# Differential attention scores as 64-row products, the two components in the two halves of the array

## The chip, the cores and the metric

The kernel runs on one core of one Trainium2 chip. The metric is the time of one execution on the device in microseconds (us). A core has TensorE for matrix products, VectorE and ScalarE for element-wise work, GpSimd, and queues that start DMA transfers. In profiles TensorE's matmuls are "PE", its weight loads "PEld", VectorE is "DVE", ScalarE is "ACT", GpSimd is "POOL" and SyncE, which starts most DMAs, is "SP".

## The reference

A two-layer encoder trunk on 256 tokens of width 2048, in float32. Each layer normalises `x`, projects it with `w_in`, mixes it in three groups of heads (a gated convolution, differential attention, and cross-attention into 256 memory tokens), and adds the result times `w_out` to `x`. The change concerns the differential attention, 6 heads with two components of 64 columns each:

```python
q = rmsnorm(d_q.reshape(b, s, DIFF_HEADS, 2, DIFF_HALF_DIM), diff_q_norm_g[l])
k = rmsnorm(d_k.reshape(b, s, DIFF_HEADS, 2, DIFF_HALF_DIM), diff_k_norm_g[l])
...
sc = jnp.einsum('bhcqd,bhckd->bhcqk', qi, kt).astype(jnp.float32) * scale + bias[None, :, None]
p = jax.nn.softmax(sc, axis=-1).astype(vt.dtype)
o = jnp.einsum('bhcqk,bhkd->bhcqd', p, vt)
return o[:, :, 0] - lam.astype(o.dtype) * o[:, :, 1]
```

The sum over `d` of the scores has only 64 terms, separately for each component `c`.

## The kernel before

**Products in parts.** Every large product is made from two tiles per operand: `hi`, the operand cast to the matmul type, and `lo`, what the cast left out. `products` (line 305) issues three matmuls per tile of 128 rows: high by high, high by low, low by high. ScalarE makes `hi` (line 294), VectorE makes `lo` (line 295). These run in `block`, which walks over 16 row tiles of a weight matrix in 8 chunks of two and accumulates two tiles of 128 tokens x 512 columns in PSUM.

**The order of work.** Tracing goes through the blocks of `w_in` one after the other. Everything else is written as generators ("tasks"): after every chunk `run_side` steps those that are due. A number that a generator yields is the count of chunks until its next step. What has been produced is noted in the set `made`, and tasks that need it wait by yielding. `keep_in_program_order` (`pin`) puts an instruction behind the one traced before it on its engine; instructions that are not pinned may be reordered when the program is laid out.

**From projection to transposed parts.** For the first three blocks of group D (q and k of all heads), `normed` scales the accumulators, and the task `qk_T` turns the result so that channels lie on partitions: `turn_sheet` gives `whole`, whose 128 partitions are, for one head, the 64 channels of component 0 and below them the 64 of component 1. `qk_T` then writes the parts of q and k into `yT`, a tile of 2 x 16 x 256 on 128 partitions that later holds the layer's mixed output. It does so for each component `c` on 64 partitions at a time: for q the high part on the component's own half and the low part on the other half; for k the high part on both halves, and the low part on both halves, in `yT` for heads 0 to 3 and in a tile of its own, `k2` (tag `bgT`), for heads 4 and 5. Lines 551 and 552 make q's parts, lines 563 and 564 k's high part twice, lines 568 and 570 k's low part and its copy to the other half.

**Scores.** `diff_scores` makes one head: two PSUM tiles `s[0]` and `s[1]` (pool `ps_s`, two buffers), one for each component, of 128 queries x 2 x 256 keys. Since q's 128 partitions are high above low, and k's are the same part twice, one matmul of 128 rows adds two products: line 626 is (q high + q low) by k high, line 627 (q high + q low) by k low. Each is one weight load of 128 x 128 and 256 moving columns; a head takes 8. Afterwards VectorE adds the position bias to `s[0]` and `s[1]` (line 631), and ScalarE takes the exponentials (line 637). Heads go in pairs (`pair`), begun every `PAIR_EVERY` = 9 chunks from the fifth block of group D on, so their matmuls fall between those of line 305. Line 519 (`weighted`) multiplies the transposed weights with `v`, in matmuls of 128 moving columns. Line 134 transposes a 32-row tile of constants at the very start, and line 763 transposes 128-row tiles of the memory tokens.

Of the kernel before, what the change touches and what calls it, by code (L numbers as in the profile page):

```python
# [10 lines left out]
F32 = mybir.dt.float32  # L11
F32R = mybir.dt.float32r
I32 = mybir.dt.int32
AF = mybir.ActivationFunctionType
ALU = mybir.AluOpType
# [3 lines left out]
P = 128  # L19
D_MODEL = 2048  # L20
SEQ = 256
DEPTH = 2
NT = SEQ // P
# [4 lines left out]
CG = W_CONV // P  # L28
DH = W_DIFF // P
HALF = 64  # L30
# [18 lines left out]
def encoder(ctx: ExitStack, tc: tile.TileContext, x, mem, norm_g, w_in, conv_w, conv_b,  # L49
            dq_g, dk_g, lq1, lk1, lq2, lk2, head_g, mem_norm_g, w_mem_kv, mq_g, mk_g, w_out, out):  # L50
    nc = tc.nc
    x, mem, out = x[0], mem[0], out[0]

    def pool(name, bufs, space=None):
        kw = {"space": space} if space is not None else {}
        return ctx.enter_context(tc.tile_pool(name=name, bufs=bufs, **kw))
# [4 lines left out]
    keep = pool("keep", 1)  # L61
# [9 lines left out]
    def nm(s):  # L71
        uid[0] += 1
        return f"{s}_{uid[0]}"
# [71 lines left out]
    kgain = const.tile([P, DEPTH], F32, name="kgain")  # L145
# [64 lines left out]
    side, tasks = deque(), []  # L210
# [3 lines left out]
    def later(g, n):  # L214
        due[id(g)] = chunk[0] + n
        return g
# [235 lines left out]
    def normed(acc, gs, st, home):  # L452
        return normed_steps(nc.vector, acc, gs, st, home)
# [13 lines left out]
    def sheets(tag):  # L467
        return lambda: sheet(tmp if tag == "e" else keep, tag)
# [56 lines left out]

    def q_parts(yT, c, h):
        return yT[:, c, h, :]

    def k_first(yT, c, h):
        return yT[:, c, CG + h, :]

    def k_second(yT, k2, c, h):
        return yT[:, c, CG + DH + h, :] if h < 4 else k2[:, c, h - 4, :]

    ROWS = (slice(0, HALF), slice(HALF, P))

    def qk_T(l, yT, k2, nat, q, k):

        whole = yield from turn_sheet(nat)

        pin = tc.keep_in_program_order
        if q is not None:
            c0, h0, nh = q
            a = c0 // P
            for c in range(2):
                own, other = ROWS[c], ROWS[1 - c]
                src = whole[own, a:a + nh, :]
                hi = yT[own, c, h0:h0 + nh, :]  # L550
                pin(nc.scalar.copy(hi, src))
                pin(nc.vector.tensor_tensor(yT[other, c, h0:h0 + nh, :], src, hi.bitcast(F32), ALU.subtract))
                yield
            made.update(("q", l, h) for h in range(h0, h0 + nh))
        if k is not None:
            c0, h0, nh = k
            a = c0 // P
            for c in range(2):
                own, other = ROWS[c], ROWS[1 - c]
                src = whole[own, a:a + nh, :]  # L560
                g = kgain[own, l:l + 1]
                hi = yT[own, c, CG + h0:CG + h0 + nh, :]
                pin(nc.scalar.activation(hi, src, AF.Copy, scale=g))
                pin(nc.scalar.activation(yT[other, c, CG + h0:CG + h0 + nh, :], src, AF.Copy, scale=g))
                for at, n, dst, d0 in ((0, min(nh, 4 - h0), yT, CG + DH + h0), (4 - h0, h0 + nh - 4, k2, 0)):
                    if n > 0:
                        lo = dst[own, c, d0:d0 + n, :]
                        pin(nc.vector.scalar_tensor_tensor(lo, whole[own, a + at:a + at + n, :], g,
                                                           hi[:, at:at + n].bitcast(F32), ALU.mult, ALU.subtract))
                        pin(nc.scalar.copy(dst[other, c, d0:d0 + n, :], lo))  # L570
                yield
            made.update(("k", l, h) for h in range(h0, h0 + nh))

    scored = set()
# [41 lines left out]
            yield 1  # L616
        held["yn"] -= 1

    def diff_scores(l, h, yT, k2):
        while not {("q", l, h), ("k", l, h)} <= made:  # L620
            yield 1
        s = [ps_s.tile([P, NT, SEQ], F32, tag="s", name=nm("s")) for _ in range(2)]
        for c in range(2):
            for i in range(NT):
                qi = q_parts(yT, c, h)[:, i * P:(i + 1) * P]
                nc.tensor.matmul(s[c][:, i, :], qi, k_first(yT, c, h), start=True, stop=False)  # L626
                nc.tensor.matmul(s[c][:, i, :], qi, k_second(yT, k2, c, h), start=False, stop=True)  # L627
        scored.add((l, h))
        e = tmp.tile([P, 2, NT, SEQ], F32, tag="e", name=nm("e"))
        for c in range(2):  # L630
            nc.vector.scalar_tensor_tensor(e[:, c], dist, -slopes[h], s[c], ALU.mult, ALU.add)  # L631
        mx = small.tile([P, 2, NT], F32, tag="mx", name=nm("mx"))
        nc.vector.tensor_reduce(mx, e, AX.X, ALU.max, negate=True)  # L633
        sm = small.tile([P, 2, NT], F32, tag="sm", name=nm("sm"))
        for c in range(2):
            for i in range(NT):
                nc.scalar.activation(e[:, c, i], e[:, c, i], AF.Exp, bias=mx[:, c, i:i + 1],  # L637
                                     accum_out=sm[:, c, i:i + 1])
        iv = small.tile([P, 2, NT], F32, tag="iv", name=nm("iv"), bufs=6)
        nc.vector.reciprocal(iv, sm)  # L640
        cf = small.tile([P, NT], F32, tag="cf", name=nm("cf"))
        nc.vector.scalar_tensor_tensor(cf, sm[:, 0], neglam[:, l:l + 1], iv[:, 1], ALU.mult, ALU.mult)
        for i in range(NT):
            nc.vector.scalar_tensor_tensor(e[:, 0, i], e[:, 1, i], cf[:, i:i + 1], e[:, 0, i], ALU.mult, ALU.add)
        return e[:, 0], iv
        yield
# [183 lines left out]
    pin = tc.keep_in_program_order  # L830
# [205 lines left out]
    s = 1  # L1036
    while s < DEPTH * KT:
        l, k = divmod(s, KT)
# [22 lines left out]
        s = group[-1] + 1  # L1061

    for l in range(DEPTH):
        st = stats_of(ssx, "st")
# [3 lines left out]

        yT = T_tile("yT")
        yTs[l] = yT  # L1070
        k2 = keep.tile([P, 2, DH - 4, SEQ], F32R, tag="bgT", name=nm("k2"))

        def x_block(cols, order=ALLK, **how):
            return block(xT, w_in[l], cols, order, rows=x_row_tiles, **how)
# [1 line left out]
        def begin_pair(n, p):  # L1076
            tasks.append(later(p, max(1, start + PAIR_EVERY * n - chunk[0])))
# [4 lines left out]
        for b in order:  # L1082
            if b in begun:
                acc = x_block([(C_D + b * NB, NB)], ALLK[-QT:], acc=begun[b])
            else:
                acc = x_block([(C_D + b * NB, NB)], ready=m.ready if l == 0 and b == order[0] else None)
            if b == 3:
                v = keep.tile([P, NT, W_DIFF], F32, tag="v", name=nm("v"))
                ga = keep.tile([P, NT, W_DIFF], F32, tag="ga", name=nm("ga"))
            if b == 4:  # L1090
                start = chunk[0]
                for n in range(DH // 2):
                    begin_pair(n, pair((2 * n, 2 * n + 1), lambda h: diff_scores(l, h, yT, k2),
                                       (lambda h, yn, po, iv: diff_out(h, yn, po, iv, st, ga),
                                        lambda h, y: split_T(yT, CG + h, y, hgain[:, l:l + 1], pin=True)), v))
            if b < 3:
                tasks.append(later(qk_T(l, yT, k2, normed(acc, HALF, st, sheets(("mqT", "mga", "e")[b])),
                                 (0, 0, 4) if b == 0 else (0, 4, 2) if b == 1 else None,
                                 (256, 0, 2) if b == 1 else (0, 2, 4) if b == 2 else None), 8))
            else:  # L1100
                for t in range(NT):
                    if b == 3:
                        nc.scalar.activation(v[:, t, 0:NB], acc[t], AF.Copy, scale=col(st, R, t))
                    elif b == 4:
                        nc.scalar.activation(v[:, t, NB:768], acc[t][:, 0:256], AF.Copy, scale=col(st, R, t))
                        silu2(ga[:, t, 0:256], acc[t][:, 256:512], st, t)
                    else:
                        silu2(ga[:, t, 256:768], acc[t], st, t)

        mqT = keep.tile([P, MH, SEQ], F32, tag="mqT", name=nm("mqT"))  # L1110
        mga = sheet(keep, "mga")
        acc = x_block([(C_M, NB)])
# [7 lines left out]
        acc = x_block([(C_M + W_MEM, NB)])  # L1120
        for t in range(NT):
            a = tmp.tile([P, NB], F32, tag="nat", name=nm("a"), bufs=3)
# [10 lines left out]
        bgT = None  # L1133
# [53 lines left out]
        acc = x_block([(C_B, NB)])  # L1187
        scaled(both_rows(bg, 0, 4), acc, HR2)
        acc = x_block([(C_B + NB, 256), (C_G + NB, 256)])
        scaled(both_rows(bg, 4, 6), [a[:, 0:256] for a in acc], HR2)  # L1190
        gate(NB, 256, [a[:, 256:512] for a in acc])
        acc = x_block([(C_G, NB)])
        gate(0, NB, acc)
        tasks.append(later(turn_bg(list(range(CG))), 9))
        acc = x_block([(C_X, NB)])
        ux = sheet(keep, "bgx", CG)
        scaled(both_rows(ux, 0, 4), acc, R2)
        acc = x_block([(C_C, NB)])
# [13 lines left out]
        acc = x_block([(C_X + NB, 256), (C_C + NB, 256)])  # L1212
# [80 lines left out]
        acc = block(yT, w_out[l], [(3 * NB, NB)], rest, apart=4 if final else 0, acc=far, opened=(True, False))  # L1293
# [32 lines left out]
```

## Time and profile before

| | |
|---|---|
| time, median of 3 runs | 919.0 us (918.97 to 920.56) |
| the profiled execution: its own time | 919.16 us |
| the profiled execution: its span | 917.4 us |
| TensorE busy | 911.9 us, 4161 matmuls |
| TensorE weight loads busy | 757.3 us, 4161 loads |
| VectorE busy | 720.1 us, 1293 instructions |
| ScalarE busy | 515.8 us, 798 instructions |
| mean DMA rate | 235 GB/s |

The span runs from the first to the last instruction of the profiled execution. Busy time is the time in which at least one instruction of an engine was in progress; matmuls are pipelined, so each one's recorded length overlaps the next, and the time it really takes from the stream is the distance between starts. In the rows of groups the columns are line, engine, operation, tiles (written <- read), shape, count | busy time in us, mean length of one in ns | idle time before them in us and what ended it. In rows of the timeline they are start and length in us, engine, line, operation, tiles, shape, count. In rows of waits they are the total in us, the number of times, and the longest.

### The profile page before, as it was taken

The page shows a single profiled execution, that of the slowest core. Times are in us where ns is not written, and L with a number is a line of the kernel's source. Part 1 is how long each engine was busy: PE and PEld are TensorE (multiplying, and loading weights), DVE is VectorE, ACT ScalarE, POOL GpSimd, SP SyncE. Part 2 cuts the span into 40 slices and gives each one's busy share as a digit, 9 for nine tenths or more (in the row PEclk, how much of TensorE's full clock was granted, in tenths as well). Part 3 has the DMA queues.
Part 4 walks back from the last instruction along what each step waited for, and adds up shares of the span by engine and source line. Part 5 has one row for each costly group of instructions (what it writes and reads, how often), then busy time and mean ns, then how long its engine had stood idle before and what let it go on. Part 6 is the DMA issues. An engine that isn't in the chain of part 4 may idle for free.

```text
span 917.4 us, 12407 instructions
## 1 busy us (share of the span) xinstructions
PE 911.9 (99%) x4161; PEld 757.3 (83%) x4161; DVE 720.1 (78%) x1293; ACT 515.8 (56%) x798; POOL 38.3 (4%) x68
## 2 busy tenths in 40 slices
PE   9999999999999999999999999999999999999998
PEld 6888888888888888888888888888888888888887
DVE  5579978857799697677789857878898787588786
ACT  5667645675555556445556544578555565546352
POOL 2435010000000000000000000000000000000000
PEclk9999999999999999999999999999999999999999
DMA  8899878886679998979777867986889998968842
GB/s 288 289 243 248 287 247 229 244 222 197 188 206 238 247 256 235 263 243 241 264 215 228 275 203 213 268 239 178 236 231 221 266 260 227 268 215 234 275 161 92
DMA packets 244560, 215.15 MB, mean 235 GB/s; under 512 B 131976, under 2 KB 171720, under 8 KB 244496
## 3 DMA queue, kind: packets, MB, share of 16 engines
q1 hardware_dynamic: 239520, 208.71, 79.3%
q0 software_dynamic: 3776, 4.59, 2.1%
q10 hardware_dynamic: 1200, 1.07, 0.3%
q8 instruction: 32, 0.52, 0.2%
q14 instruction: 32, 0.26, 0.1%
HBM read 193.30 MB, written 21.00 MB: 234 GB/s over the span
## 4 chain that ended last, share of the span: by engine, by line
PE 99%; DMA 0%; ACT 0%; SPq 0%; DVE 0%; issue 0%; ACTq 0%
PE acc L305 92%; PE x L351 2%; PE po L519 1%; PE acc L351 1%; PE s L627 1%; PE po L749 1%; PE s L626 1%; PE acc L933 1%; PE pt L763 0%; DMA raw<-in_w_mem_kv_dram 0%; PE s L683 0%; PE s L681 0%; PE s L682 0%; PE rest L305 0%; ACT hi L915 0%; SPq L833 0%
## 5 line engine op out<-in xcount | busy, mean ns | idle before, releaser
L305 PE MATMUL acc<-hi,xT 128*128 128x512 f32 x1792 | 558.4, 390 | 0.0
L294 ACT CAST hi<-raw 128x1024 fp32r<-128x1024 f32 x270 | 283.9, 1053 | 277.3 <-PE acc L305 200.0
L295 DVE TENSOR_TENSOR lo<-raw,hi 128x1024 fp32r<-128x1024 f32 x270 | 329.0, 1222 | 126.7 <-ACT hi L294 124.5
L305 PEld LDWEIGHTS acc<-hi,xT 128*128 128x128 f32 x1792 | 336.3, 188 | 69.0
L305 PE MATMUL acc<-lo,xT 128*128 128x512 f32 x896 | 349.2, 390 | 0.0
L305 PEld LDWEIGHTS acc<-lo,xT 128*128 128x128 f32 x896 | 168.2, 188 | 33.6
L305 PE MATMUL acc<-hi,yT 128*128 128x512 f32 (+1 forms) x432 | 134.1, 388 | 0.0
L305 PEld LDWEIGHTS acc<-hi,yT 128*128 128x128 f32 x432 | 81.0, 188 | 16.7
L305 PE MATMUL acc<-lo,yT 128*128 128x512 f32 x216 | 83.7, 388 | 0.0
L305 PE MATMUL acc<-hi,memT 128*128 128x512 f32 x248 | 78.0, 392 | 0.0
L305 PEld LDWEIGHTS acc<-hi,memT 128*128 128x128 f32 x248 | 46.2, 188 | 9.3
L916 DVE SCALAR_TENSOR_TENSOR lo<-raw,cva,hi 128x1024 fp32r<-128x1024 f32 (+1 forms) x34 | 41.0, 1218 | 15.4 <-ACT hi L915 15.1
L305 PE MATMUL acc<-lo,memT 128*128 128x512 f32 x124 | 48.0, 391 | 0.0
L305 PEld LDWEIGHTS acc<-lo,yT 128*128 128x128 f32 x216 | 40.6, 188 | 8.4
L915 ACT ACTIVATE hi<-raw,cva 128x1024 fp32r<-128x1024 f32 (+1 forms) x34 | 36.5, 1101 | 12.4 <-DMA raw<-in_w_mem_kv_dram 12.2
L305 PEld LDWEIGHTS acc<-lo,memT 128*128 128x128 f32 x124 | 23.3, 188 | 5.5 <-DVE lo L916 0.8
L377 ACT CAST hi<-wide 128x1024 fp32r<-128x1024 f32 x15 | 15.6, 1050 | 16.3 <-DVE wide L380 6.9
L637 ACT ACTIVATE e<-e,mx 128x256 f32<-128x256 f32 x48 | 23.8, 500 | 1.4 <-DVE mx L633 1.3
L780 POOL DMA_DIRECT2D xt<-in_x_dram x32 | 21.5, 678 | 19.7 <-DVE rsy L189 13.6
L377 DVE TENSOR_TENSOR lo<-wide,hi 128x1024 fp32r<-128x1024 f32 x15 | 18.1, 1220 | 3.5 <-ACT hi L377 3.3
L264 ACT ACTIVATE xT<-xf,gx 128x256 fp32r<-128x256 f32 x32 | 14.3, 503 | 5.7 <-DVE xf L786 5.0
L631 DVE SCALAR_TENSOR_TENSOR e<-dist,s 128x512 f32<-128x512 f32 x24 | 15.7, 680 | 2.2 <-PE s L627 1.7
(210 smaller groups left out, 765.8 us busy)
## 6 DMA issues: line engine op xcount, KB each, us to landing
raw<-in_w_in_dram SPq DMA_DIRECT2D x192, 512.0 KB, 4.6
raw<-in_w_out_dram SPq DMA_DIRECT2D x54, 512.0 KB, 4.8
raw<-in_w_in_dram SPq DMA_DIRECT2D x64, 256.0 KB, 4.3
raw<-in_w_mem_kv_dram SPq DMA_DIRECT2D x30, 512.0 KB, 6.4
d<-sh SPq DMA_DIRECT2D x88, 128.0 KB, 4.2
sh<-d SPq DMA_DIRECT2D x72, 128.0 KB, 4.1
wide<-in_w_out_dram SPq DMA_DIRECT2D x10, 512.0 KB, 7.0
xs<-in_x_dram SPq DMA_DIRECT2D x4, 512.0 KB, 6.3
```

The source lines that it names most:

```text
L264: both = (nc.scalar.activation(hi, src, AF.Copy, scale=gain), nc.vector.scalar_tensor_tensor(lo, src, gain, hi.bitcast(F32), ALU.mult, ALU ...
L294: nc.scalar.copy(hi, raw)
L295: nc.vector.tensor_tensor(lo_, raw, hi.bitcast(F32), ALU.subtract)
L305: i = nc.tensor.matmul(acc, left, right, start=start, stop=stop)
L351: nc.tensor.matmul(acc, left[a], right[b], start=first and i == 0, stop=last and i == 2)
L377: return ((hi, pin(nc.scalar.copy(hi, src))), (lo, pin(nc.vector.tensor_tensor(lo, src, hi.bitcast(F32), ALU.subtract))))
L519: nc.tensor.matmul(po[:, t, :], eT[:, i, t, k, :], v[:, k, h * P:(h + 1) * P], start=k == 0, stop=k == NT - 1)
L631: nc.vector.scalar_tensor_tensor(e[:, c], dist, -slopes[h], s[c], ALU.mult, ALU.add)
L637: nc.scalar.activation(e[:, c, i], e[:, c, i], AF.Exp, bias=mx[:, c, i:i + 1], accum_out=sm[:, c, i:i + 1])
L780: tc.keep_in_program_order(nc.gpsimd.dma_start(st[:, n], src[n * B:(n + 1) * B].rearrange("p (b r) -> b p r", b=NA)))
L915: both = (nc.scalar.activation(hi[:, j], raw[:, j], AF.Copy, scale=g), nc.vector.scalar_tensor_tensor(lo[:, j], raw[:, j], g, hi[:, j].bit ...
L916: nc.vector.scalar_tensor_tensor(lo[:, j], raw[:, j], g, hi[:, j].bitcast(F32), ALU.mult, ALU.subtract))
```

## The change

`qk_T` writes q's high part to `yT[:, 0, h]` and its low part to `yT[:, 1, h]`, and k's likewise at index `CG + h`, in one instruction each over all 128 partitions, so that component 0 lies on partitions 0 to 63 and component 1 on 64 to 127. The part on the other half, the copies and the tile `k2` go, and with them one of the two `yield`s for q and one of the two for k. `diff_scores` forms each score tile from three products (high by high, high by low, low by high), the two components alternating: 12 matmuls of 64 rows a head, all pinned.

```diff
--- before.py
+++ after.py
@@ -525,50 +525,30 @@
 
 
 
-    def q_parts(yT, c, h):
-        return yT[:, c, h, :]
-
-    def k_first(yT, c, h):
-        return yT[:, c, CG + h, :]
-
-    def k_second(yT, k2, c, h):
-        return yT[:, c, CG + DH + h, :] if h < 4 else k2[:, c, h - 4, :]
-
     ROWS = (slice(0, HALF), slice(HALF, P))
 
-    def qk_T(l, yT, k2, nat, q, k):
+    def qk_T(l, yT, nat, q, k):
 
         whole = yield from turn_sheet(nat)
 
         pin = tc.keep_in_program_order
         if q is not None:
             c0, h0, nh = q
-            a = c0 // P
-            for c in range(2):
-                own, other = ROWS[c], ROWS[1 - c]
-                src = whole[own, a:a + nh, :]
-                hi = yT[own, c, h0:h0 + nh, :]
-                pin(nc.scalar.copy(hi, src))
-                pin(nc.vector.tensor_tensor(yT[other, c, h0:h0 + nh, :], src, hi.bitcast(F32), ALU.subtract))
-                yield
+            src = whole[:, c0 // P:c0 // P + nh, :]
+            hi = yT[:, 0, h0:h0 + nh, :]
+            pin(nc.scalar.copy(hi, src))
+            pin(nc.vector.tensor_tensor(yT[:, 1, h0:h0 + nh, :], src, hi.bitcast(F32), ALU.subtract))
+            yield
             made.update(("q", l, h) for h in range(h0, h0 + nh))
         if k is not None:
             c0, h0, nh = k
-            a = c0 // P
-            for c in range(2):
-                own, other = ROWS[c], ROWS[1 - c]
-                src = whole[own, a:a + nh, :]
-                g = kgain[own, l:l + 1]
-                hi = yT[own, c, CG + h0:CG + h0 + nh, :]
-                pin(nc.scalar.activation(hi, src, AF.Copy, scale=g))
-                pin(nc.scalar.activation(yT[other, c, CG + h0:CG + h0 + nh, :], src, AF.Copy, scale=g))
-                for at, n, dst, d0 in ((0, min(nh, 4 - h0), yT, CG + DH + h0), (4 - h0, h0 + nh - 4, k2, 0)):
-                    if n > 0:
-                        lo = dst[own, c, d0:d0 + n, :]
-                        pin(nc.vector.scalar_tensor_tensor(lo, whole[own, a + at:a + at + n, :], g,
-                                                           hi[:, at:at + n].bitcast(F32), ALU.mult, ALU.subtract))
-                        pin(nc.scalar.copy(dst[other, c, d0:d0 + n, :], lo))
-                yield
+            src = whole[:, c0 // P:c0 // P + nh, :]
+            g = kgain[:, l:l + 1]
+            hi = yT[:, 0, CG + h0:CG + h0 + nh, :]
+            pin(nc.scalar.activation(hi, src, AF.Copy, scale=g))
+            pin(nc.vector.scalar_tensor_tensor(yT[:, 1, CG + h0:CG + h0 + nh, :], src, g, hi.bitcast(F32),
+                                               ALU.mult, ALU.subtract))
+            yield
             made.update(("k", l, h) for h in range(h0, h0 + nh))
 
     scored = set()
@@ -616,15 +596,15 @@
             yield 1
         held["yn"] -= 1
 
-    def diff_scores(l, h, yT, k2):
+    def diff_scores(l, h, yT):
         while not {("q", l, h), ("k", l, h)} <= made:
             yield 1
         s = [ps_s.tile([P, NT, SEQ], F32, tag="s", name=nm("s")) for _ in range(2)]
-        for c in range(2):
-            for i in range(NT):
-                qi = q_parts(yT, c, h)[:, i * P:(i + 1) * P]
-                nc.tensor.matmul(s[c][:, i, :], qi, k_first(yT, c, h), start=True, stop=False)
-                nc.tensor.matmul(s[c][:, i, :], qi, k_second(yT, k2, c, h), start=False, stop=True)
+        for i in range(NT):
+            for n, (a, b) in enumerate(((0, 0), (0, 1), (1, 0))):
+                for c, rows in enumerate(ROWS):
+                    pin(nc.tensor.matmul(s[c][:, i, :], yT[rows, a, h, i * P:(i + 1) * P], yT[rows, b, CG + h, :],
+                                         start=n == 0, stop=n == 2))
         scored.add((l, h))
         e = tmp.tile([P, 2, NT, SEQ], F32, tag="e", name=nm("e"))
         for c in range(2):
@@ -1068,7 +1048,6 @@
 
         yT = T_tile("yT")
         yTs[l] = yT
-        k2 = keep.tile([P, 2, DH - 4, SEQ], F32R, tag="bgT", name=nm("k2"))
 
         def x_block(cols, order=ALLK, **how):
             return block(xT, w_in[l], cols, order, rows=x_row_tiles, **how)
@@ -1090,11 +1069,11 @@
             if b == 4:
                 start = chunk[0]
                 for n in range(DH // 2):
-                    begin_pair(n, pair((2 * n, 2 * n + 1), lambda h: diff_scores(l, h, yT, k2),
+                    begin_pair(n, pair((2 * n, 2 * n + 1), lambda h: diff_scores(l, h, yT),
                                        (lambda h, yn, po, iv: diff_out(h, yn, po, iv, st, ga),
                                         lambda h, y: split_T(yT, CG + h, y, hgain[:, l:l + 1], pin=True)), v))
             if b < 3:
-                tasks.append(later(qk_T(l, yT, k2, normed(acc, HALF, st, sheets(("mqT", "mga", "e")[b])),
+                tasks.append(later(qk_T(l, yT, normed(acc, HALF, st, sheets(("mqT", "mga", "e")[b])),
                                  (0, 0, 4) if b == 0 else (0, 4, 2) if b == 1 else None,
                                  (256, 0, 2) if b == 1 else (0, 2, 4) if b == 2 else None), 8))
             else:
```

## The prediction

> **What bounds the kernel now.** I read the engine table first, then the chain that ended last, then the list of what TensorE waits for, and only then the rows around the edit. The page and the two views:
>
> ```profile
> span 917.4 us, 12407 instructions
> PE 911.9 (99%) x4161; PEld 757.3 (83%) x4161; DVE 720.1 (78%) x1293; ACT 515.8 (56%) x798; POOL 38.3 (4%) x68
> PEclk9999999999999999999999999999999999999999
> PE 99%; DMA 0%; ACT 0%; SPq 0%; DVE 0%; issue 0%; ACTq 0%
> by line: PE acc L305 91.7%; PE x L351 1.5%; PE po L519 1.2%; PE acc L351 1.1%; PE s L627 0.6%; PE po L749 0.6%; PE s L626 0.6%; PE acc L933 0.5%; PE pt L763 0.4%; DMA raw<-in_w_mem_kv_dram 0.4%; PE s L683 0.2%; PE s L681 0.2%; PE s L682 0.2
> PE warm L128 <- DVE zeros L123: 1.2, 1, 1.2
> PE acc L933 <- ACT hi L915: 0.8, 1, 0.8
> ```
>
> TensorE is busy for 99% of the span at full granted clock, and all but a rounding of the chain is its own. Its whole list of waits is two rows, 1.2 and 0.8 us, both at the start. The kernel is one unbroken stream of matmuls, and its time is the sum of their slots: the distance from one start to the next, not the recorded length, which overlaps its neighbours. The differential scores, lines 626 and 627, are 0.6% + 0.6% of the chain, some 11 us of 917.4. The most this edit could ever win is that.
>
> The slots, from the timeline of TensorE (start, length, line) and, below the "...", of its weight loads, at the first head of layer 0:
>
> ```profile
> 210.05 0.39 PE L305 MATMUL acc<-hi,xT 128*128 128x512 f32 x1
> 210.28 0.28 PE L627 MATMUL s<-yT 128*128 128x256 f32 x1
> 210.39 0.28 PE L626 MATMUL s<-yT 128*128 128x256 f32 x1
> ...
> 210.99 0.28 PE L627 MATMUL s<-yT 128*128 128x256 f32 x1
> 211.11 0.40 PE L305 MATMUL acc<-hi,xT 128*128 128x512 f32 x1
> 211.34 0.40 PE L305 MATMUL acc<-lo,xT 128*128 128x512 f32 x1
> ...
> 210.28 0.19 PEld L626 LDWEIGHTS s<-yT 128*128 128x128 f32 x1
> 210.39 0.19 PEld L627 LDWEIGHTS s<-yT 128*128 128x128 f32 x1
> ```
>
> Seven score matmuls lie between 210.28 and 211.11, so one slot of 256 columns is 0.83/7 = 0.119 us; a slot of 512 columns is 0.23. Neighbouring kinds of matmul cost each other nothing: 210.05 to 210.28 is an ordinary 0.23 slot, 210.99 to 211.11 an ordinary 0.12. The loads show why a new stationary tile per matmul is free here: each starts as a matmul starts and belongs to the one after it.
>
> The groups by form give the counts:
>
> ```profile
> L626 PE MATMUL s<-yT 128*128 128x256 f32 x48 | 12.3, 286 | 0.0
> L627 PE MATMUL s<-yT 128*128 128x256 f32 x32 | 8.1, 283 | 0.0
> L627 PE MATMUL s<-k,yT 128*128 128x256 f32 x16 | 3.9, 280 | 0.0
> L626 PEld LDWEIGHTS s<-yT 128*128 128x128 f32 x48 | 9.1, 189 | 0.5
> ```
>
> 48 + 32 + 16 = 96 matmuls: 12 heads (6 in each of 2 layers) of 8. 96 x 0.119 = 11.4 us, which agrees with the 1.2% of the chain.
>
> **TensorE's part of the change.** A head becomes 12 matmuls instead of 8: two row tiles, three products, two components, each on 64 rows. In all 144 instead of 96, with 144 weight loads. They are pinned in an order that alternates the halves, rows 0 to 63 and then 64 to 127, and the two halves write different PSUM tiles (`s[0]`, `s[1]`). So everything hangs on whether the two halves of a pair run at the same time. No full stretch of the trace shows 64-row matmuls; the bounds from the nearest rows:
>
> - Halves of a pair in one slot: 72 slots x 0.119 = 8.6 us, 2.8 less than now.
> - Halves one after the other: 144 x 0.119 = 17.1 us, 5.7 more.
>
> I take the first, as a guess that the rows don't exclude: the two halves read different partitions, use different rows and write different tiles, and the stream above shows the array already starting a load and a matmul at the same instant. Nothing in the rows shows a resource of a 64-row matmul that its partner needs too, except perhaps the load path, which is a rival below. "Different tiles can execute LdWeights and Matmul in parallel", says the Trainium skill (TensorEngine Tiling (Array Packing), section Tiling Modes, Key Properties); no run here shows it yet.
>
> The change between 128-row and 64-row work is a second unknown: twice a head, 24 times. Its lower end is the ordinary boundary above, nothing. Its upper end is that the array must empty first: a 512-column matmul lasts 0.40 where its slot is 0.23, so 0.17 of tail would be laid bare on entry; 0.28 less 0.12 is 0.16 on exit. The one place where the row count changes now is the single 32-row transpose at the start:
>
> ```profile
> 3.01 0.18 PEld L134 LDWEIGHTS pva<-ident,va 32*128 32x128 f32 x1 [0.83 <-issue]
> 3.01 0.31 PE L134 MATMUL pva<-ident,va 32*128 32x32 f32 x1
> 3.25 0.29 PEld L763 LDWEIGHTS pt<-ident,xs 128*128 128x128 f32 x2
> 3.25 0.69 PE L763 MATMUL pt<-ident,xs 128*128 128x128 f32 x2
> ```
>
> The 128-row load that follows starts at 3.25, while the 32-row matmul ends at 3.01 + 0.31 = 3.32: the load, at least, is not held back until the array is empty. That is nearer to the lower end, so I take 10 ns a change, an estimate between nothing and that end: 24 x 0.01 = 0.24 us. Sum for TensorE: -2.8 + 0.2 = -2.6 us.
>
> **ScalarE's and VectorE's part.** `qk_T` now writes hi and lo on all 128 rows at once. Its present work, by form:
>
> ```profile
> L551 ACT CAST yT<-sh 64x1024 fp32r<-64x1024 f32 x4 | 4.2, 1046 | 0.0
> L551 ACT CAST yT<-sh 64x512 fp32r<-64x512 f32 x4 | 2.5, 620 | 0.0
> L563 ACT ACTIVATE yT<-sh,kgain 64x1024 fp32r<-64x1024 f32 x4 | 4.6, 1150 | 0.1
> L563 ACT ACTIVATE yT<-sh,kgain 64x512 fp32r<-64x512 f32 x4 | 2.9, 719 | 0.0
> L564 ACT ACTIVATE yT<-sh,kgain 64x1024 fp32r<-64x1024 f32 x4 | 4.6, 1152 | 0.1
> L564 ACT ACTIVATE yT<-sh,kgain 64x512 fp32r<-64x512 f32 x4 | 2.9, 725 | 0.1
> L570 ACT CAST yT<-yT 64x512 fp32r<-64x512 f32 x8 | 5.0, 621 | 0.2
> L570 ACT CAST k<-k 64x512 fp32r<-64x512 f32 x4 | 2.5, 615 | 0.0
> L552 DVE TENSOR_TENSOR yT<-sh,yT 64x1024 fp32r<-64x1024 f32 x4 | 4.9, 1220 | 0.1
> L552 DVE TENSOR_TENSOR yT<-sh,yT 64x512 fp32r<-64x512 f32 x4 | 2.7, 686 | 0.1
> L568 DVE SCALAR_TENSOR_TENSOR yT<-sh,kgain,yT 64x512 fp32r<-64x512 f32 x8 | 6.0, 745 | 0.1
> L568 DVE SCALAR_TENSOR_TENSOR k<-sh,kgain,yT 64x512 fp32r<-64x512 f32 x4 | 3.0, 746 | 0.0
> ```
>
> ScalarE: line 564 goes (4.6 + 2.9 = 7.5), line 570 goes (5.0 + 2.5 = 7.5), lines 551 and 563 halve, taking 128 rows at the length of 64 (half of 4.2 + 2.5 + 4.6 + 2.9 = 14.2, so 7.1): 22.1 us less. VectorE: line 552 halves (3.8 less); line 568's 12 become 2 of 512 and 2 of 1024, by the rows 2 x 0.75 + 2 x 1.22 = 3.9 instead of 9.0, so 5.1 less: together 8.9. On the path all of this is worth nothing: in the two rows of TensorE's waits no line of `qk_T` stands, and the 91.7% on line 305 is never late for its parts. Cover gone would change that only the other way, and here the covered work shrinks. With one `yield` less for q and one for k, heads are marked ready a step or two earlier; scores then take slots earlier, but the number of slots is the same. `k2` goes, a tile whose slot later tiles of tag `bgT` share; nothing waits for that now. No DMA and no queue is touched.
>
> One wait gets longer. VectorE's line 631 adds the bias from `s[0]` and then `s[1]`; now `s[0]` is whole after four matmuls (0.48 us), afterwards only at the end of the 12. Queued behind it on VectorE are the lo parts of the weights (line 295). At worst that is 0.4 us a head on an engine that is idle for 22% of the span, and TensorE has no wait for VectorE but the one at the start. I cost it at nothing; without that cover it would be 12 x 0.4 = 4.8 us.
>
> **Sum.** The profiled execution took 919.16 us (span 917.4 and 1.76 around it); 919.16 - 2.6 = 916.6. It lies 0.16 above the median of the three runs, 919.0, so against the median the forecast is about 916.4; I keep 916.5 between them.
>
> **The rivals.**
>
> *The array empties at each change of row count.* The halves overlap, but 24 changes cost 0.16 to 0.17 each: 24 x 0.165 = 4.0, so -2.8 + 4.0 = +1.2, 920.3 us. For it: the tails are in every row above, and a stream of equal matmuls cannot show whether a change would lay them bare. Against it: the load at 3.25. With half the tail it is 918.3. From 0.12 a change on nothing is won. If the first load after a change could not be hidden either, 0.19 more each way by the loads' row, it is 24 x 0.19 = 4.6 on top, 924.9. The Trainium skill has this rule: "Changing tiling mode (not just tile) drains the TensorE" (TensorEngine Tiling (Array Packing), section Tiling Modes, Key Properties). By that rule the time is 920.3 us, by the load at 3.25 it is 916.6. The load there did not wait for the drain; whether the matmul did, this trace cannot show.
>
> *The weight loads take turns: slower.* Matmuls of the two halves overlap, the loads do not. Now 8 loads a head hide behind 256 columns each; 12 loads would have only 6 slots to hide behind. How close loads can follow each other shows where matmuls are short, in `weighted`:
>
> ```profile
> 257.83 1.06 PE L519 MATMUL po<-v,sh 128*128 128x128 f32 x8
> L519 PE MATMUL po<-v,sh 128*128 128x128 f32 x96 | 12.7, 275 | 0.0
> ```
>
> Eight in 1.06 with the last lasting 0.275: (1.06 - 0.275)/7 = 0.112 a slot, though they stream half of 256 columns; half of 0.119 would be 0.06. So something other than streaming sets it, and the load is the candidate. A 64-row load has the same 128 columns. Then 144 x 0.112 = 16.1, 4.7 more than now: 923.9 us. It decides as soon as one load takes more than half of a 0.119 slot and cannot run beside the other half's load. Against it: the halves' loads read and write different rows.
>
> *The change doesn't do what it says.* The halves run in turn, 5.7 more: 924.9 us. For it: no row shows two matmuls of this kind at once. With the tails of the first rival as well, 928.9.
>
> **How the numbers follow.** About 0.2% (1.8 us) is what a measurement of this kernel can tell from no change: its three runs lie 918.97 to 920.56 apart. The forecast (halves overlap, changes up to 0.04 each, so 916.3 to 917.3) gets 0.42. Halves overlap but changes cost part or all of the tail, 917.3 to 920.8: 0.20. Loads in turn, 923.9: 0.20. Halves in turn, or the changes with tail and load bare, near 924.9: 0.12. Both together, up to 929: 0.06. So faster 0.42, same 0.20, slower 0.38. The likeliest case's own range is 916.0 to 917.3; the range for 8 in 10 reaches over the drain and up to the loads in turn and the halves in turn: 916.0 to 925.2.
>
> **What would show it.** Right: in the timeline the two halves of a pair start within a few hundredths of each other and pairs are 0.12 apart; a head takes 0.72 us from its first start to the next line-305 matmul; TensorE's waits remain the two at the start; ScalarE's busy time is about 494 and VectorE's 711. Loads in turn: starts evenly 0.11 apart, as on line 519. Halves in turn: evenly 0.12 apart. Drain: the first 64-row matmul and the first line-305 matmul after the head come 0.16 late. Wrong altogether: a new wait of TensorE for hi or lo parts, or score matmuls scattered among those of line 305, so that halves lose their partners.

## The result, and the profile after

The changed kernel takes 923.68 us (median of 5 runs, 922.97 to 924.52), the kernel before beside it 919.22 us (918.97 to 920.56). The ratio is 1.0047, with a 95% interval of 1.0033 to 1.0062: 4.5 us slower, where 2.6 us faster was forecast. The time lies inside the range given, on the other side of no change.

The head of the page after, its list of TensorE's waits, and the scores' group by form:

```profile
span 922.4 us, 12464 instructions
PE 917.2 (99%) x4209; PEld 755.4 (82%) x4209; DVE 713.4 (77%) x1281; ACT 494.0 (54%) x770; POOL 38.2 (4%) x68
PEclk9999999999999999999999999999999999999999
...
PE warm L128 <- DVE zeros L123: 1.2, 1, 1.2
PE acc L913 <- ACT hi L895: 0.4, 1, 0.4
...
L606 PE MATMUL s<-yT 64*128 64x256 f32 x144 | 14.0, 299 | 0.0
```

The frame of the argument held. TensorE is busy 99% of the span at full granted clock, and its waits are still the two at the start. ScalarE fell from 515.8 to 494.0 us and VectorE from 720.1 to 713.4, and none of that reached the end. The span grew by 5.0 us, TensorE's busy time by 5.3, so the time was lost inside TensorE's stream, in rows that are counted as busy. The timeline shows where, first matmuls and then weight loads, at the first head of layer 0:

```profile
209.56 0.39 PE L305 MATMUL acc<-lo,xT 128*128 128x512 f32 x1
209.78 0.39 PE L305 MATMUL acc<-hi,xT 128*128 128x512 f32 x1
210.10 0.97 PE L606 MATMUL s<-yT 64*128 64x256 f32 x12
211.00 0.50 PE L305 MATMUL acc<-hi,xT 128*128 128x512 f32 x1
211.34 0.40 PE L305 MATMUL acc<-lo,xT 128*128 128x512 f32 x1
...
209.56 0.19 PEld L305 LDWEIGHTS acc<-hi,xT 128*128 128x128 f32 x1
210.10 0.77 PEld L606 LDWEIGHTS s<-yT 64*128 64x128 f32 x12 [0.35 <-issue]
211.00 0.19 PEld L305 LDWEIGHTS acc<-hi,xT 128*128 128x128 f32 x1
211.11 0.19 PEld L305 LDWEIGHTS acc<-lo,xT 128*128 128x128 f32 x1
```

The halves do overlap: 12 matmuls start and end within 0.97 us, which 12 slots of 0.119 one after the other would not fit into. The loss is at the two ends. On the way in, the slot that begins at 209.78 lasts 0.32 instead of 0.23, so 0.09 is spent with nothing new starting. Then the first 64-row load begins only at 210.10, with its matmul; in the rows of the kernel before, a load began with the matmul ahead of its own. On the way out, the last pair starts at about 210.80 (0.97 after 210.10, less the 0.27 that one matmul lasts) and its slot ends at 210.92; the load for line 305 begins 0.08 later, at 211.00, again together with its matmul, and that slot is 0.34 instead of 0.23. From 209.78 to 211.34 is 1.56 us. Two slots of line 305 (0.454) and six pair slots of 0.118 (0.706) account for 1.16; the remaining 0.40 us is what I call a **visit**: one stay in 64-row work, in and out.

There are also more visits than heads. In the timeline around the second head:

```profile
217.07 0.39 PE L305 MATMUL acc<-hi,xT 128*128 128x512 f32 x1
217.39 0.38 PE L606 MATMUL s<-yT 64*128 64x256 f32 x1
217.70 0.50 PE L305 MATMUL acc<-hi,xT 128*128 128x512 f32 x1
218.03 0.40 PE L305 MATMUL acc<-lo,xT 128*128 128x512 f32 x1
218.36 0.62 PE L606 MATMUL s<-yT 64*128 64x256 f32 x6
```

One score matmul stands alone, matmuls of line 305 were laid out behind it, and the other 11 follow at 218.36 (this view ends within them). The same cut comes at the second head of all six pairs: 18 visits instead of 12, and 7 slots instead of 6 in each cut head, since the lone matmul and its partner no longer share one. The sum: 18 x 0.40 = 7.2, plus (72 + 6) x 0.118 = 9.2, together 16.4 us against 11.4 before: 5.0 more, the growth of the span. Worked out in the same way at every visit of this trace, the cost is 0.39 to 0.41 us each time and 7.2 us for all 18.

### The profile page after: what moved, and what is told of

It reads as the page before. It is cut to its first block, busy times and chain, and to the rows that moved or that the text cites. A ratio compares the mean times of both kernels' runs of the same rounds, so it can differ in the third digit from the quotient of the medians.

```text
span 922.4 us, 12464 instructions
## 1 busy us (share of the span) xinstructions
PE 917.2 (99%) x4209; PEld 755.4 (82%) x4209; DVE 713.4 (77%) x1281; ACT 494.0 (54%) x770; POOL 38.2 (4%) x68
## 4 chain that ended last, share of the span: by engine, by line
PE 99%; ACT 0%; DVE 0%; issue 0%
PE acc L305 92%; PE x L351 1%; PE s L606 1%; PE po L519 1%; PE acc L351 1%; PE po L729 1%; PE acc L913 1%; PE pt L743 0%; PE s L663 0%; PE s L661 0%; PE s L662 0%; PE warm L128 0%; PE rest L305 0%; ACT hi L895 0%; DVE xs L1211 0%; ACT memT L261 0%
## 5 line engine op out<-in xcount | busy, mean ns | idle before, releaser
L895 ACT ACTIVATE hi<-raw,cva 128x1024 fp32r<-128x1024 f32 (+1 forms) x34 | 36.4, 1099 | 11.7 <-DMA raw<-in_w_mem_kv_dram 11.4
L481 DVE STREAM_TRANSPOSE sh<-sh 128x1024 f32<-128x1024 f32 (+2 forms) x14 | 17.3, 1238 | 0.0
```

The costliest lines, as they stand in the source:

```text
L481: tc.keep_in_program_order(nc.vector.transpose(src, src))
L895: both = (nc.scalar.activation(hi[:, j], raw[:, j], AF.Copy, scale=g), nc.vector.scalar_tensor_tensor(lo[:, j], raw[:, j], g, hi[:, j].bit ...
```

## The experiments

The theory after this reading: a visit costs 0.40 us whatever is done in it, a pair of halves 0.118. Rivals: the cost lies in each 64-row matmul or load, or in the changed order of the other engines.

**e1: no cut heads.** In `pair`, the second head comes one chunk later:

```diff
             es.append((yield from begin(h)))
-            yield 2
+            yield 3
```

> The changed kernel with the second head of a pair one chunk later, so that no head's 12 matmuls are cut in 1 + 11: 12 visits to 64-row work instead of 18, the same 144 matmuls. Theory (a visit costs 0.40 us: wait for the array to empty plus an unhidden load, on the way in and on the way out; a pair of halves 0.118): 12 x 0.40 + 72 x 0.118 = 13.3 against 11.4, so 1.9 above the kernel before, about 921.1. Rival (the cost lies in each 64-row matmul or load, not in the visit): same 144, so it stays near 923.7. Rival (the cost lies elsewhere, in the changed order of ScalarE and VectorE): near 923.7 too.

Measured 921.35 us against 918.95, ratio 1.0025 (1.0016 to 1.0034): 2.4 more than before, where theory said 1.9. All heads are whole, and the second looks like the first:

```profile
218.65 0.39 PE L305 MATMUL acc<-hi,xT 128*128 128x512 f32 x1
218.97 0.97 PE L606 MATMUL s<-yT 64*128 64x256 f32 x12
219.87 0.50 PE L305 MATMUL acc<-hi,xT 128*128 128x512 f32 x1
```

The same 144 matmuls, with the same work on the other engines, give back some 2 of the 4.5 us. The cost goes with the visits.

**e2: both heads of a pair in one visit.** Scores of both heads are issued in one run of 24, the second head's two tiles from the pool `ps_t`; the third pair begins 6 chunks later, so that its run stays whole (no run shows it without that). A pair now begins when the parts of both heads are there and nothing is held in `held["e"]`. The main lines:

```diff
+        s = {h: [pl.tile([P, NT, SEQ], F32, tag=tag, name=nm("s")) for _ in range(2)]
+             for h, (pl, tag) in zip(heads, ((ps_s, "s"), (ps_t, "t")))}
+        for h in heads:
+            for i in range(NT):
...
-            tasks.append(later(p, max(1, start + PAIR_EVERY * n - chunk[0])))
+            tasks.append(later(p, max(1, start + PAIR_EVERY * n + 6 * (n == 2) - chunk[0])))
```

> The changed kernel with both heads of a pair scored in one run of 24 matmuls (the second head's tiles from the other PSUM pool, the third pair 6 chunks later): 6 visits. Theory (0.40 a visit): 6 x 0.40 + 8.5 = 10.9 against 11.4, so 0.5 below the kernel before, about 918.7. Rival (cost by the matmul): near 923.7. A new wait of TensorE for the PSUM tiles would lie above 918.7 by as much as its row says.

Measured 918.91 us against 918.95, ratio 0.9999 (0.9990 to 1.0008). No loss is left that these runs could tell from nothing.

```profile
209.85 0.39 PE L305 MATMUL acc<-hi,xT 128*128 128x512 f32 x1
210.17 1.69 PE L609 MATMUL s<-yT 64*128 64x256 f32 x24
211.78 0.50 PE L305 MATMUL acc<-hi,xT 128*128 128x512 f32 x1
212.12 0.40 PE L305 MATMUL acc<-lo,xT 128*128 128x512 f32 x1
...
PE acc L305 <- DVE lo L295: 0.4, 1, 0.4
```

From 209.85 to 212.12 is 2.27; less 0.454 and 12 x 0.118, a visit of 24 costs 0.40, the same as a visit of 12 and, below, of one. By the visits 0.5 us should have been won; the profile has a wait of 0.4 on VectorE's lo part that the kernel before does not have, and half a microsecond is inside the interval. Whether it is a gain of 0.5 cannot be said.

**e3: the halves in turn.** As e1, with the loop over the components outside:

```diff
-        for i in range(NT):
-            for n, (a, b) in enumerate(((0, 0), (0, 1), (1, 0))):
-                for c, rows in enumerate(ROWS):
+        for c, rows in enumerate(ROWS):
+            for i in range(NT):
+                for n, (a, b) in enumerate(((0, 0), (0, 1), (1, 0))):
```

> As e1, but a head's 12 matmuls run through component 0 first and component 1 afterwards, so that neighbours use the same half of the array. Theory: no overlap, 144 slots of 0.118 = 17.0, and 12 visits of 0.40 = 4.8: 21.8 against 11.4, about 929.6. Rival (alternating is not what makes halves overlap): as e1, about 921.1. Rival (a load cannot be drawn ahead of a matmul on the same rows): slots of 0.21 or more, 144 x 0.21 = 30, above 938.

Measured 925.25 us against 918.95, ratio 1.0066 (1.0053 to 1.0079): 6.3 more than before, not 10.4. My expectation missed. In the timeline:

```profile
208.79 0.39 PE L305 MATMUL acc<-hi,xT 128*128 128x512 f32 x1
209.11 1.32 PE L606 MATMUL s<-yT 64*128 64x256 f32 x12
210.36 0.50 PE L305 MATMUL acc<-hi,xT 128*128 128x512 f32 x1
```

From 209.11 to 210.36 is 1.25; in the run of e1 that stretch is 0.90 with 6 slots. The 0.35 more are 3 slots, so 9 in all and not 12. Counting the matmuls in progress in stretches of one slot (columns: stretch, its length, TensorE's busy time and its count, that of the loads and their count, clock, DMA share and rate; the first stretch is longer by the first load) shows the second half coming in early:

```profile
209.08:209.32 0.24, 0.21 (x1) 0.21 (x2) 1.00 0.33 120
209.32:209.44 0.12, 0.12 (x2) 0.12 (x2) 1.00 0.09 34
209.44:209.56 0.12, 0.12 (x4) 0.12 (x3) 1.00 0.05 18
209.56:209.67 0.11, 0.11 (x4) 0.11 (x4) 1.00 0.09 36
209.67:209.78 0.12, 0.12 (x5) 0.12 (x4) 1.00 0.05 18
209.78:209.90 0.12, 0.12 (x6) 0.12 (x3) 1.00 0.09 36
209.90:210.02 0.12, 0.12 (x5) 0.12 (x2) 1.00 0.04 17
```

One matmul starts in the first stretch, one more in the second, and two in the third, though the program issues six of one half before the first of the other. Then one starts in the fourth, two each in the fifth and sixth, and one each in the last three: 12 in 9 slots. The second of the pair in the third stretch lasts 0.38 us and its load starts together with it, at 209.45, as at the start of a visit. I read it as the first matmul of the second half; its load stands in front of it, and the half has no start in the fourth stretch. With 9 slots the sum is 12 x (9 x 0.118 + 0.40) = 17.5, 6.1 more than before, close to the 6.3 measured.

**e8: twelve in turn**, made to settle that miss. As e2, but the 12 matmuls of component 0 of both heads come before the 12 of component 1:

```diff
-        for h in heads:
-            for i in range(NT):
-                for n, (a, b) in enumerate(((0, 0), (0, 1), (1, 0))):
-                    for c, rows in enumerate(ROWS):
+        for c, rows in enumerate(ROWS):
+            for h in heads:
+                for i in range(NT):
+                    for n, (a, b) in enumerate(((0, 0), (0, 1), (1, 0))):
```

> As e2 (both heads in one run of 24, 6 visits), but the 12 matmuls of component 0 of both heads come first, then the 12 of component 1. e3 took 9 slots for 6 + 6, with the first matmul of the second half starting beside the fourth of the first half. If TensorE looks ahead over a fixed number of instructions, the second half again starts 3 matmuls early: 24 - 3 = 21 slots a pair, 6 x (21 x 0.118 + 0.41) = 17.3 against 11.4, 5.9 above the kernel before. If the overlap is in proportion: 18 slots, 3.8 above. If e3's gain had another cause and nothing overlaps: 24 slots, 8.1 above.

Measured 924.74 us against 918.88, ratio 1.0061 (1.0044 to 1.0077): 5.9 more than before, as a fixed look-ahead would have it. (By the rows of e3 the second half begins there beside the third matmul of the first, not beside the fourth as the expectation says; the three shared slots are right.)

```profile
210.18 2.75 PE L609 MATMUL s<-yT 64*128 64x256 f32 x24
212.87 0.50 PE L305 MATMUL acc<-hi,xT 128*128 128x512 f32 x1
```

2.69 from start to exit, against 1.61 in e2 with 12 slots: 1.08 more are 9 slots, so 21 = 24 - 3. The pattern is that of e3: at 211.24, beside the ninth of the 12, a matmul of 0.38 us starts together with its load, with three of the first half still to come. So the second half starts early by the same count whether 6 or 12 stand before it. Other counts were not run.

**e4 to e7: the visit by itself.** These leave the scores of the kernel before as they are and put one or two matmuls ahead of each head's 8:

```diff
         s = [ps_s.tile([P, NT, SEQ], F32, tag="s", name=nm("s")) for _ in range(2)]
+        for _ in range(1):
+            for c, rows in enumerate(ROWS):
+                pin(nc.tensor.matmul(s[c][:, 0, :], yT[rows, 0, h, 0:P], yT[rows, 0, CG + h, :],
+                                     start=True, stop=True))
```

`ROWS` is (0 to 63, 64 to 127) in e4; both entries are 0 to 127 in e5 and 0 to 95 in e6; e7 has the one entry 0 to 63.

> The kernel before with one extra pair of 64-row matmuls ahead of each head's 8 (they write to the score tiles and are overwritten by the real products); nothing else is changed. Theory: 12 visits of 0.40 + 12 pair slots of 0.118 = 6.2, about 925.4. Rival (cost by the matmul, 4.5 us over 144 of them): 24 matmuls cost 0.75 beside their slots, 919.2 + 1.4 + 0.75 = 921.4. Rival (no cost of 64-row work at all, the loss of the change is elsewhere): 919.2 + 1.4 = 920.6.

> The control of e4: the kernel before with two extra matmuls of all 128 rows ahead of each head's 8 (overwritten by the real products). Theory (only 64-row work makes a visit): 24 slots of 0.119 = 2.9, about 921.8. Rival (extra pinned matmuls disturb the stream whatever their rows): near e4, 925.3.

> As e5, but the two extra matmuls use rows 0 to 95. If the visit is a change of the array's division (64-row halves against the whole), 96 rows are no visit: 2.9, about 921.8. If any change of the number of rows in use costs a visit: 2.9 + 12 x 0.40 = 7.7, about 926.7.

> The kernel before with one extra matmul of rows 0 to 63 ahead of each head's 8 (overwritten by the real products). Theory: a visit costs the same for one half as for a pair, 12 x (0.40 + 0.118) = 6.2, about 925.2, as e4. Rival (the cost comes from two halves at work together): 12 x 0.118 = 1.4, about 920.4.

| extra per head | us | before, same chip | difference | ratio (95%) | expected |
|---|---|---|---|---|---|
| e4: a pair of 64 rows | 925.32 | 918.95 | 6.4 | 1.0069 (1.0056 to 1.0081) | 6.2 |
| e5: two of 128 rows | 922.22 | 918.40 | 3.8 | 1.0040 (1.0025 to 1.0055) | 2.9 |
| e6: two of 96 rows | 922.14 | 918.40 | 3.7 | 1.0039 (1.0024 to 1.0054) | 2.9 |
| e7: one of 64 rows | 925.57 | 918.40 | 7.2 | 1.0076 (1.0059 to 1.0093) | 6.2 |

In e4 one of the 12 pairs (the sixth head of layer 0) was laid out in 1 + 1 with a 128-row matmul between, so it has 13 visits, not 12: 13 x (0.40 + 0.118) = 6.7 against the 6.4 measured.

One 64-row matmul of 256 columns costs as much as a pair, and more than two matmuls that use twice its rows. The three rows that show the ends of each, e4, e6 and e7 in this order:

```profile
209.87 0.39 PE L305 MATMUL acc<-hi,xT 128*128 128x512 f32 x1
210.19 0.38 PE L625 MATMUL s<-yT 64*128 64x256 f32 x2
210.50 0.38 PE L630 MATMUL s<-yT 128*128 128x256 f32 x1
```

```profile
209.67 0.39 PE L305 MATMUL acc<-hi,xT 128*128 128x512 f32 x1
209.89 0.40 PE L625 MATMUL s<-yT 96*128 96x256 f32 x2
210.13 0.28 PE L630 MATMUL s<-yT 128*128 128x256 f32 x1
```

```profile
209.65 0.39 PE L305 MATMUL acc<-hi,xT 128*128 128x512 f32 x1
209.96 0.38 PE L625 MATMUL s<-yT 64*128 64x256 f32 x1
210.28 0.38 PE L630 MATMUL s<-yT 128*128 128x256 f32 x1
```

In e4 and e7 the slot before the 64-row work is 0.31 to 0.32, and the first matmul of each kind lasts 0.38 instead of 0.28: its load stands in front of it. In e6 two 96-row matmuls lie in ordinary slots, 0.24 for both. Over the whole traces, each of e7's 12 visits costs 0.39 beside its slot, and no stay in e6 costs more than 0.01. So it isn't any change in the number of rows that costs; 64 rows cost and 96 don't. The medians of e5 to e7 lie 0.8 to 1.0 us above the expectations. The intervals hold the expected figures (2.3 to 5.1 us for e5, 2.2 to 5.0 for e6, 5.4 to 8.5 for e7), so that excess is not clear of the noise; whether it is more than noise is open.

## Why the prediction was wrong

**What bounds the kernel: right.** The kernel is TensorE's stream, and only slots count. The 22.1 and 8.9 us taken from ScalarE and VectorE were worth nothing on the path. (The rows of `qk_T` became 22.2 and 8.8 us shorter; the busy times fell by 21.8 and 6.7.) The longer wait of VectorE for the score tiles, costed at nothing, made no new wait of TensorE.

**The halves overlap: right,** at the slot taken, 0.118 a pair. The two rivals that denied it, loads in turn and halves in turn, are out, although the first gave 923.9 us, within 0.3 of the time measured. A time that fits is not yet a cause; the timeline separated them at once.

**The change between 128-row and 64-row work: the step that failed.** I put 10 ns on each of 24 changes, 0.24 us in all. Measured: 0.20 on each of 36, 7.2 us. A whole head took 0.90 us from its first start to the next matmul of line 305 (210.10 to 211.00), not 0.72. Two parts of the step were wrong.

The price. I leaned on one row, the 32-row transpose at the start, and on its load that "is not held back until the array is empty". That load began together with its own matmul at 3.25, not one matmul ahead, and this is what an unhidden load looks like. Whether the row change or its data held it back there, the row cannot say; it was no evidence for a free change, and I took it for that. The upper end that I had set out, the tail laid bare, and the bare load that the rival added to it were of the right kind. Its size here is 0.08 to 0.09 until the next load begins and 0.11 for that load, in and out alike. The Trainium skill has the rule that changing the tiling mode drains TensorE (TensorEngine Tiling (Array Packing), Tiling Modes, Key Properties). The 0.09 on the way in fits it, but no row shows that the array is empty by then: the load begins at 210.10, and by its recorded length the last 128-row matmul ends at 209.78 + 0.39 = 210.17. The load laid bare behind it, the larger half, showed only in the rows. It may not belong to the change of rows alone, since in e3 and e8 a load stood bare in the middle of 64-row work.

The count. I took 12 heads for 12 visits. In the kernel before, the first head was already cut in 1 + 7, the lone one 2.4 us ahead of the seven that the prediction shows:

```profile
207.87 0.28 PE L626 MATMUL s<-yT 128*128 128x256 f32 x1
```

Another head, in layer 1, was cut in 4 + 2 + 2. There a cut costs nothing. I counted seven where there should be eight and did not ask what a cut would cost when each is a visit. Scattered score matmuls stood among the signs of being wrong, without a price. With whole heads (e1) the sum would have been 12 x 0.40 - 2.8 = 2.0 more than before, still slower.

**The rival of the draining array** named the right mechanism and gave 920.3 us, or 924.9 with bare loads. I gave the first 0.20 and the second a share of 0.12, and let the weak row decide against both. That was a misjudgement of evidence, not of arithmetic. That 924.9 comes so near to 923.68 is partly luck: it has 24 changes at 0.355, 8.5 us, where 36 at 0.20, 7.2 us, were measured, so that a price too high and a count too low nearly cancel. It is luck too where the range holds the time on account of halves or loads in turn, which did not happen.

## What to carry to other kernels

In these runs two 64-row products at once took one slot instead of two, but each stay in 64-row work cost about 0.40 us in a stream of 128-row matmuls: collect them into few long runs, look in the laid-out order whether something was slipped in between, and count visits before counting slots. Here a head saves 8 x 0.119 - 6 x 0.118 = 0.24 us, so by these slots one visit must serve two heads before it pays, and with two (e2) no gain clear of the noise was measured. When a single odd row is the only evidence for a cost, compare it with the steady stream (when does the load begin?) and not with its own length.

## What the runs showed of the hardware

- 96 rows are no visit and 64 rows are: two 96-row matmuls ran in slots of 0.12 among 128-row ones (e6), a single 64-row matmul cost 0.39 beside its slot (e7).
- TensorE overlaps the halves without an alternating program: with 6 or 12 matmuls of one half issued before the other, the second half started with three of the first still to come in both (e3 and e8, 9 and 21 slots). For 12 matmuls, alternating (6 slots) is still worth 3 of the 9.
- Loads of one half followed each other at 0.118 a matmul in e3, on the same rows, so neither the same rows nor the pinned order holds a load back there. Bare were the first loads after a change between 128 and 64 rows (0.11 us each), and one load in the middle of 64-row work in e3 and e8, read above as the first of the second half.
